# V scaled when it comes back for the spatial product, in odd tiles; two operands of the output weights kept raw and split in phase two; the slots set anew

## The chip, the cores and the metric

One core of a Trainium2 chip runs one launch of the kernel. The metric is the device time of that launch in microseconds. Three runs of the kernel before gave 757.01, 755.66 and 757.59; the median is 757.01.

## The reference

One decoder layer on x of 2048 tokens by 1024 channels, in float32. Cut to what matters here:

```python
h = rms_norm(x, pre_norm_g)
a_u, a_v, sq, sk, sv, mq, z = split(h @ w_in)          # 512, 512, 256, 128, 128, 256, 1024 columns
# A: spatial gating; per token and group of 128 channels
vg = (gelu(a_v) - mean) * rsqrt(var + EPS) * v_g + v_b
sv = einsum('gts,bnsgc->bntgc', tril(w_s), vg) + b_s    # chunks of 128 tokens, 4 groups
y_a = gelu(a_u) * sv
y_b = sliding_window_attention(sq, sk, sv, sinks, rel_bias)   # 4 heads, window 128
y_c = memory_cross_attention(mq, mem_k, mem_v)                # 4 heads, 256 memory tokens
y = concat(y_a, y_b, y_c) * silu(z)
out = x + rms_norm(y @ w_out, post_norm_g)
```

## The kernel before

Every float32 product is made of three products of rounded parts: an operand `w` is kept as a rounded part (ScalarE's cast) and the rest (VectorE's subtraction), and TensorE adds up rounded times rounded and the two cross terms. The helper `split` (lines 144 to 148) makes the two parts; a half-megabyte block of weights thus becomes a megabyte.

**Phase one** takes the tokens in four tiles of 512 (t = 0 to 3). A tile projects V (four products into four PSUM banks, line 1133), then the values and keys of the window attention, q, the memory q and half of the gates z (`group`, line 443). The weights come through a ring of three buffers, loaded already split from DRAM (`split_d`, line 242) after the first tile. After V, line 1151 applies gelu, `bn_stats` gathers mean and variance of each token and group, `scale_and_shift` (lines 296 to 305) turns them into a scale `rv` and a shift `nb` (with a power on GpSimd, line 302), and 16 ScalarE instructions of 128x128 per tile (line 1158) apply them; the result goes to DRAM as `vhat_d` (line 1160). The copy of the values out of PSUM (line 1181) comes after that.

The odd tiles end with `set_a`: a Strassen scheme over two tiles and two blocks of columns makes u and half of z for both tiles at once (28 products of 12 matmuls, line 878). In between, `ahead` loads V back from DRAM for one tile and group (line 857), and `spatial` multiplies it with the spatial weights (`mix`, line 844).

**The output weights.** In tile 2, `weight_operands` loads the four blocks of the output weights, for each half j, makes the seven operands of a second Strassen scheme (B11, T1, B22, T3, T2, B21, T4), splits each in two 512-column pieces (lines 763 to 764) and stores the 2 MB of each operand (both halves) to `wo_d`. T4 is the difference of block 21 and T2; B21 is block 21 itself.

**Phase two** (from line 1243) multiplies y by these operands, two tiles at a time, seven products in each pass, each of four steps (m) of 12 matmuls (line 1443). `work` holds, by step, what else is to be done: loads of y and of operands (`weights`, line 1356), sums, and the splits of y (`rounded` on ScalarE, line 1295, ahead of the bank's own work; `rest` on VectorE, line 1300, behind it). In the first pass the third product, at steps 8 to 11, uses B21, and the sixth, at steps 20 to 23, uses T4.

**What sets the order.** TensorE's and SyncE's (DMA) queues run in program order. In phase one the other engines' order comes from the scheduler's simulated time line. Phase one is cut into slots of six large matmuls (`slot`, line 1036); slot 0 of a tile comes after V, the values, the keys and the first q, 28 slots into the tile. The tables at the head of the file say at which slot of its tile each job is written into the program: MIX_SLOTS (load and spatial product), A_STARTS, A_TURN, A_END (the three stages of each attention unit), WO_SLOTS and WO_LOADS (output weights), H_SUMS, H_LOADS, H_OPS (operands of the first Strassen scheme), and others. In phase two all queues are in program order.

Of the kernel before, what the change touches and what calls it, by code (L numbers as in the profile page):

```python
# [32 lines left out]
W_OPS = ("B11", "B21", "B22", "T1", "T2", "T3", "T4")  # L33
STORE_AFTER = 5

LATE = ((U_Z + 6, 0), (U_Z + 7, 0), (U_V, 1), (U_V + 1, 1), (U_V + 2, 1))

TURN_SLOT = 21

PRE = 28  # L40
N_SLOTS = (36, 84, 28, 84)
BASE = tuple(sum(N_SLOTS[:t]) + PRE * (t + 1) for t in range(NT))
STATS = ((-10, -4, 3, 2, 5, 5, 8, 10), (18, 24, 28, 30, 31, 38, 39, 41), (-22, -20, -17, -10, -9, -5, -2, 1))
SQUARES = ((2, 2, 6, 10, 9, 14, 14, 15),
           (19, 25, 31, 33, 35, 42, 41, 46),
           (-21, -14, -15, -10, -4, -3, 4, 2))
RSTD = ((15, 22, 23), (50, 55, 55), (6, 10, 12))
# [3 lines left out]
LOADS = ((22, 23, 17, 31, 33), (65, 66, 66, 66, 67), (4, 10, 18, 19, 24, 23, 28, 31))
MAKES = ((29, 30, 30, 32, 31, 31, 44, 36),
         (69, 68, 69, 76, 76, 78, 89, 90),
         (16, 16, 21, 22, 24, 25, 30, 36))
A_STARTS = ((10, 16, 21, 26, 35, 38, 41, 44, 47, 50, 53, 58),
# [3 lines left out]
A_TURN = ((6, 8, 11, 8, 11, 8, 5, 8, 10, 9, 11, 6),  # L59
# [3 lines left out]
A_END = ((13, 13, 14, 13, 17, 10, 11, 11, 8, 11, 9, 11),  # L63
# [3 lines left out]

# [6 lines left out]
SEQ_A = tuple((op, g) for op in FIRST_OPS for g in range(4)) + LAST_SEQ  # L74
MIX_SLOTS = ((51, 58), (49, 61), (59, 63), (62, 68), (62, 70), (67, 73), (68, 74), (73, 80))
W_ORDER = ("B11", "T1", "B22", "T3", "T2", "B21", "T4")
WO_SLOTS = ((4, 13, 13, 15, 18, 21, 29), (34, 41, 46, 51, 58, 63, 68))
WO_LOADS = ((-1, 3, 2, 16), (31, 29, 33, 56))
T_SLOTS = (-24, -13, -9, 4)
T_TILES = (1, 1, 1, 1)  # L80
T_STEPS = ((1, 4, 4, 8, 8), (2, 8, 8, 9, 10), (0, 2, 6, 8, 9), (3, 5, 7, 9, 9))
H_SUMS = (((-15, -14, -13, -15, -9, -7, -13, -7, -7, -6, -5),
# [7 lines left out]
H_SPARE = ((-8, 6), (22, 25))  # L90
H_LOADS = (((28, 30, 32, 37), (43, 47, 47, 48), (44, 47, 49, 53)),
           ((33, 37, 38, 35), (33, 39, 38, 41), (49, 49, 46, 56)))
H_OPS = (((35, 38, 37, 42), (54, 56, 53, 54), (51, 56, 53, 63)),
         ((36, 37, 42, 42), (48, 52, 53, 55), (56, 56, 57, 63)))
H_STORE = (3, 3)
Y_SUMS = ((-18, -11, -10), (-15, -8, -7))
Y_OPS = ((66, 73, 67, 79, 70), (72, 80, 80, 79, 80))
Y_WEIGHTS = (63, 81)
VALUES = (5, -4, 1, 0)
PUT_OFF = (4, 0, 3, 7, 6, 4)  # L100


@with_exitstack
def kernel(
# [33 lines left out]
    def f32(ap):  # L138
        return ap.bitcast(F32)
# [65 lines left out]
    vhat_d = dram.tile([NT, 4, P, TS], F32, name="vhat_d")  # L205
    wo_d = {op: dram.tile([2, P, 2, D], F32, name=f"wo_{op}") for op in W_OPS}
    yd = dram.tile([NT, KC, P, TS], F32, name="yd")
# [29 lines left out]
    def split_unit(i):  # L237
# [57 lines left out]
    def scale_and_shift(st, t):  # L295

        twice, apart, spread, rv = (tiny.tile([P, 16], F32, tag=f"v{n}", name=f"v{n}_{t}", bufs=1) for n in ("sum", "dif", "var", "rstd"))
        nc.vector.tensor_tensor(apart, st[:, :, 1], st[:, :, 4], ALU.subtract)
        nc.vector.scalar_tensor_tensor(spread, st[:, :, 2], P * EPS, st[:, :, 5], ALU.add, ALU.add)
        nc.vector.scalar_tensor_tensor(apart, apart, 0.25, apart, ALU.mult, ALU.mult)  # L300
        nc.vector.scalar_tensor_tensor(spread, spread, 1.0 / P, apart, ALU.mult, ALU.add)
        nc.gpsimd.tensor_tensor(rv, spread, mhalf, ALU.pow)
        nc.vector.tensor_tensor(twice, st[:, :, 1], st[:, :, 4], ALU.add)
        nc.vector.scalar_tensor_tensor(twice, twice, -0.5, rv, ALU.mult, ALU.mult)
        return rv, twice
# [442 lines left out]
    def weight_operands(j):  # L748

        r = {}  # L750
        places = ((lambda: quarter(0, 0), lambda: quarter(0, 1), lambda: quarter(1, 0), lambda: quarter(1, 1),
                   lambda: new_spare(0), lambda: new_spare(1), lambda: spare[0]),
                  (lambda: spare[1], lambda: spare[0]) * 4)[j]

# [4 lines left out]
        def operand(op, raw):  # L759
# [4 lines left out]
            store_later(wo_d[op][j], f32(w), PUT_OFF[0])  # L764

        def difference(new, a, b, at):
            r[new] = r[at]
            for c in (slice(0, 512), slice(512, D)):
                nc.vector.tensor_tensor(r[new][:, c], r[a][:, c], r[b][:, c], ALU.subtract)
# [78 lines left out]
    def set_a(p):  # L848
# [6 lines left out]
        def ahead(t, g):  # L855
            vg[t, g] = sp.tile([P, 4, P], F32, tag="L", name=f"vg_{t}_{g}", bufs=4)
            nc.sync.dma_start(vg[t, g], vhat_d[t, :, :, g * P : (g + 1) * P].rearrange("i p c -> p i c"))

        def spatial(t, g):
            gate[t, g] = sp.tile([P, TS], F32, tag="a", name=f"a_{t}_{g}", bufs=3)  # L860
            mix(t, g, vg.pop((t, g)), gate[t, g])
            if t == t1:
                times(U[g], gate[t, g])

        for n, (load_at, mix_at) in enumerate(MIX_SLOTS):
            t, g = (t1, t0)[n % 2], n // 2
            add_jobs(t1, [(load_at, lambda t=t, g=g: ahead(t, g)), (mix_at, lambda t=t, g=g: spatial(t, g))])

# [219 lines left out]
    for t in range(NT):  # L1088
# [58 lines left out]
        st = tiny.tile([P, 16, 6], F32, tag="st", name=f"st_{t}", bufs=1)  # L1147
        Gs = []
        for i in range(4):
            G = sp.tile([P, TS], F32, tag=("G", "ZB")[i // 2], name=f"G_v{t}_{i}", bufs=2)  # L1150
            gelu(vps[i], f"v{t}_{i}", G, 1.0 if t else late["rstd"][:, i : i + 1])
            for g in range(4):
                nc.vector.bn_stats(st[:, 4 * i + g, :], G[:, g * P : (g + 1) * P])
            Gs.append(G)
        rv, nb = scale_and_shift(st, t)
        for i, G in enumerate(Gs):
            for g in range(4):
                nc.scalar.activation(G[:, g * P : (g + 1) * P], G[:, g * P : (g + 1) * P], AF.Identity,  # L1158
                                     bias=nb[:, 4 * i + g : 4 * i + g + 1], scale=rv[:, 4 * i + g : 4 * i + g + 1])
# [437 lines left out]
```

## Time and profile before

| | |
|---|---|
| median of three runs | 757.01 us |
| the profiled execution | 753.89 us |
| its span, first to last instruction | 752.2 us |
| TensorE busy | 736.2 us (98%) |
| VectorE (DVE) busy | 563.8 us (75%) |
| ScalarE (ACT) busy | 475.0 us (63%) |
| GpSimd (POOL) busy | 82.8 us (11%) |
| moved by DMA | 219.92 MB, 292 GB/s over the span |

Times are microseconds from the span's start. PE is TensorE's matmuls, PEld its weight loads, SPq the DMA issues of SyncE. A row of a timeline gives the start, the duration, engine, line, operation, output and inputs, shapes, how many instructions were merged, and in brackets how long the engine was idle before it and what ended that. A row of a group gives the number of instructions, busy time, the mean duration in ns, and the idle time ahead of them.

### The profile page before, as it was taken

The page shows a single profiled execution, that of the slowest core. Times are in us where ns is not written, and L with a number is a line of the kernel's source. Part 1 is how long each engine was busy: PE and PEld are TensorE (multiplying, and loading weights), DVE is VectorE, ACT ScalarE, POOL GpSimd, SP SyncE. Part 2 cuts the span into 40 slices and gives each one's busy share as a digit, 9 for nine tenths or more (in the row PEclk, how much of TensorE's full clock was granted, in tenths as well). Part 3 has the DMA queues.
Part 4 walks back from the last instruction along what each step waited for, and adds up shares of the span by engine and source line. Part 5 has one row for each costly group of instructions (what it writes and reads, how often), then busy time and mean ns, then how long its engine had stood idle before and what let it go on. Part 6 is the DMA issues. An engine that isn't in the chain of part 4 may idle for free.

```text
span 752.2 us, 10609 instructions
## 1 busy us (share of the span) xinstructions
PE 736.2 (98%) x3612; PEld 617.3 (82%) x3612; DVE 563.8 (75%) x1001; ACT 475.0 (63%) x1044; POOL 82.8 (11%) x106
## 2 busy tenths in 40 slices
PE   8999999989999999999999999999999999999996
PEld 6888888768888888887888888888888888888884
DVE  6656897598987589833798968787689528687587
ACT  7799765885599953327668895678954234444441
POOL 1020031100230000010033010221000000010011
PEclk9999999999999999999999999999999999999999
DMA  8989877799975686899998999956577899546924
GB/s 332 360 305 392 292 308 277 272 390 384 341 271 168 221 250 199 293 373 383 367 383 320 393 306 386 377 178 192 170 254 234 284 386 404 184 174 258 352 86 195
DMA packets 80342, 219.92 MB, mean 292 GB/s; under 512 B 7548, under 2 KB 16289, under 8 KB 71841
## 3 DMA queue, kind: packets, MB, share of 16 engines
q1 hardware_dynamic: 75152, 210.27, 77.0%
q10 hardware_dynamic: 5136, 8.98, 3.2%
q8 instruction: 28, 0.46, 0.3%
q14 instruction: 26, 0.20, 0.1%
HBM read 153.16 MB, written 66.07 MB: 291 GB/s over the span
## 4 chain that ended last, share of the span: by engine, by line
PE 71%; DVE 13%; ACT 7%; DMA 6%; issue 1%; POOL 1%; ACTq 0%; DVEq 0%; SPq 0%; POOLq 0%
PE X L878 12%; PE X L1443 12%; PE g_z L443 8%; PE Y_S L1443 6%; PE v L1133 5%; PE g_mq L443 4%; PE Y L878 3%; PE g_q L443 3%; PE Y L1443 3%; ACT G_v L1158 2%; DMA s4b<-in_wst 2%; PE o_b L664 2%; PE gm L555 2%; PE l_b L632 2%; PE Z L878 1%; DVE hs L146 1%
## 5 line engine op out<-in xcount | busy, mean ns | idle before, releaser
L443 PE MATMUL g_z<-hs,ring 128*128 128x512 f32 x360 | 87.6, 394 | 0.0
L1133 PE MATMUL v<-ring,hs 128*128 128x512 f32 x336 | 81.4, 393 | 0.2 <-ACT hs L399 0.2
L443 PEld LDWEIGHTS g_z<-hs,ring 128*128 128x128 f32 x360 | 66.0, 188 | 12.7
L1133 PEld LDWEIGHTS v<-ring,hs 128*128 128x128 f32 x336 | 61.6, 188 | 13.6 <-ACT ring L145 0.6
L878 PE MATMUL X<-hs,ring 128*128 128x512 f32 x288 | 71.1, 394 | 0.0
L878 PEld LDWEIGHTS X<-hs,ring 128*128 128x128 f32 x288 | 52.6, 188 | 10.0
L443 PE MATMUL g_q<-hs,ring 128*128 128x512 f32 x192 | 46.8, 396 | 0.0
L443 PE MATMUL g_mq<-hs,ring 128*128 128x512 f32 x192 | 45.5, 391 | 0.7 <-DMA ring<-split_d 0.7
L443 PEld LDWEIGHTS g_mq<-hs,ring 128*128 128x128 f32 x192 | 35.5, 188 | 8.1 <-DMA ring<-split_d 1.1
L443 PEld LDWEIGHTS g_q<-hs,ring 128*128 128x128 f32 x192 | 35.8, 190 | 7.1
L146 DVE TENSOR_TENSOR ring<-wraw_a,ring 128x1024 fp32r<-128x1024 f32 x28 | 34.4, 1229 | 8.6 <-ACT ring L145 6.6
L1336 POOL TENSOR_TENSOR r<-a,mhalf 128x1 f32<-128x1 f32 x16 | 12.8, 801 | 221.0 <-DVE a L1334 216.3
L654 POOL TENSOR_SCALAR_AFFINE_SELECT pT_b<-pT_b 128x512 fp32r<-128x512 f32 x30 | 21.9, 730 | 133.3 <-ACT pT_b L145 133.3
L1443 PE MATMUL Y_S<-hs,yop 128*128 128x512 f32 x144 | 33.1, 389 | 0.0
L610 ACT ACTIVATE L_c<-L_c,den_c 128x256 f32<-128x256 f32 x64 | 29.1, 507 | 5.1 <-DVE den_c L608 5.1
L1443 PEld LDWEIGHTS Y_S<-hs,yop 128*128 128x128 f32 x144 | 27.0, 188 | 5.6
L146 DVE TENSOR_TENSOR ring<-wraw,ring 128x1024 fp32r<-128x1024 f32 (+1 forms) x18 | 20.9, 1162 | 13.9 <-ACT ring L145 13.7
L1304 ACT ACTIVATE junk<-oa 128x512 f32<-128x512 f32 x16 | 10.1, 633 | 33.5 <-DVE oa L1490 24.6
L1443 PE MATMUL X<-hs,ring 128*128 128x512 f32 x120 | 30.7, 391 | 0.0
L1443 PE MATMUL X<-hs,yop 128*128 128x512 f32 x120 | 30.5, 390 | 0.0
L1300 DVE TENSOR_TENSOR yop<-y,yop 128x1024 fp32r<-128x1024 f32 x10 | 12.2, 1222 | 24.0 <-ACT yop L1295 24.0
L145 ACT CAST ring<-wraw_a 128x1024 fp32r<-128x1024 f32 x28 | 29.3, 1046 | 0.0
(285 smaller groups left out, 1776.3 us busy)
## 6 DMA issues: line engine op xcount, KB each, us to landing
ring<-split_d SPq DMA_DIRECT2D x38, 1024.0 KB, 8.2
split_d<-ring SPq DMA_DIRECT2D x12, 1024.0 KB, 9.4
wraw<-in_wst SPq DMA_DIRECT2D x21, 512.0 KB, 5.8
hs<-wo_B SPq DMA_DIRECT2D x8, 1024.0 KB, 8.3
y<-yd SPq DMA_DIRECT2D x8, 1024.0 KB, 11.1
xs<-in_x SPq DMA_DIRECT2D x24, 256.0 KB, 6.7
hd_S<-h SPq DMA_DIRECT2D x24, 256.0 KB, 6.6
hrS<-hd_S SPq DMA_DIRECT2D x24, 256.0 KB, 4.6
```

The lines of the kernel that those rows point to most:

```text
L145: a = nc.scalar.copy(hi, src)
L146: b = (lo_engine or nc.vector).tensor_tensor(lo, src, f32(hi), ALU.subtract)
L443: nc.tensor.matmul(ps, w[:, wi, k * P : (k + 1) * P], h(t, hi, k), start=(n == 0), stop=(n == 3 * KC - 1))
L555: nc.tensor.matmul(ps, w[:, wi, k * P : (k + 1) * P], late["mT"](hi, k), start=(n == 0), stop=(n == 3 * KC - 1))
L610: last = nc.scalar.mul(p[:, e, :], p[:, e, :], den[:, e : e + 1])
L632: nc.tensor.matmul(lg[:, e, :], S[kv][:, e, c * P : (c + 1) * P], keys[t][:, kv, s, c * P : c * P + 256], start=(s == 0), stop=(s == 1))
L654: nc.gpsimd.affine_select(prev[:, s], f32(own[:, s]), [[0, 4], [-1, P]], ALU.is_gt, 0.0, base=0, channel_multiplier=1)
L664: nc.tensor.matmul(o[:, kv, :], SV[:, c + w, kv].rearrange("p a b -> p (a b)"), pT, start=(n == 0), stop=(n == len(terms) - 1))
L878: nc.tensor.matmul(banks[g], w[:, wi, k * P : k * P + P], at_slot(places[op], hi, k), start=first and i == 0, stop=i == 11, skip_group_che ...
L1133: nc.tensor.matmul(vps[i], h(t, hi, 2 * j + kk)[:, i * P : (i + 1) * P], w[:, wi, kk * 512 : (kk + 1) * 512], start=(j == 0 and (hi, wi, k ...
L1158: nc.scalar.activation(G[:, g * P : (g + 1) * P], G[:, g * P : (g + 1) * P], AF.Identity, bias=nb[:, 4 * i + g : 4 * i + g + 1], scale=rv[ ...
L1443: nc.tensor.matmul(banks[m], a(s, k)[:, m * P : (m + 1) * P], w(v, k), start=first and n == 0, stop=n == 11, skip_group_check=not first)
```

## The change

*V.* After gelu the tile is stored to `vhat_d` as it is. `scale_and_shift` is called after that, and its two results are kept (`moments`, with two buffers). The 16 scalings of line 1158 go from each tile; in the odd tiles a job `centred` between the load and the spatial product makes four of them for each tile and group, on the tile that was loaded back. MIX_SLOTS gets a third slot for it.

*The output weights.* B21 and T4 are no longer split in tile 2. Block 21 is copied inside DRAM at slot 45 of tile 1 (`worw_d["B21"]`, 1 MB), and the difference T4 is stored raw (1 MB). In phase two each of the two is loaded raw into the place of the rest, rounded into its own place by ScalarE, and the rest is made in place by VectorE, in two halves: B21 at steps 3 and 4, T4 at steps 17 and 18.

*Slots.* The tables of slots are set anew, some by one or two, some by more, and a store is issued six slots after it is written instead of five.

```diff
-STORE_AFTER = 5
+STORE_AFTER = 6
...
-A_END = ((13, 13, 14, 13, 17, 10, 11, 11, 8, 11, 9, 11),
-         (16, 15, 14, 16, 8, 11, 9, 11, 12, 9, 10, 11),
-         (14, 14, 13, 14, 14, 11, 9, 11, 11, 10, 10, 14),
-         (13, 13, 15, 16, 19, 14, 12, 14, 14, 12, 4, 11))
+A_END = ((14, 14, 15, 14, 18, 10, 18, 14, 10, 13, 9, 12),
+         (16, 15, 14, 16, 8, 11, 12, 12, 12, 10, 10, 11),
+         (16, 14, 13, 14, 18, 11, 9, 11, 11, 11, 10, 14),
+         (13, 13, 15, 16, 20, 13, 12, 15, 18, 12, 7, 11))
...
-MIX_SLOTS = ((51, 58), (49, 61), (59, 63), (62, 68), (62, 70), (67, 73), (68, 74), (73, 80))
-W_ORDER = ("B11", "T1", "B22", "T3", "T2", "B21", "T4")
-WO_SLOTS = ((4, 13, 13, 15, 18, 21, 29), (34, 41, 46, 51, 58, 63, 68))
-WO_LOADS = ((-1, 3, 2, 16), (31, 29, 33, 56))
+MIX_SLOTS = ((53, 56, 58),
+             (49, 59, 61),
+             (58, 61, 62),
+             (62, 63, 67),
+             (62, 68, 70),
+             (67, 67, 73),
+             (68, 72, 75),
+             (73, 77, 79))
+W_ORDER = ("B11", "T1", "B22", "T3", "T2")
+LATE_OPS = ("B21", "T4")
+COPY_SLOT = 45
+WO_SLOTS = ((4, 13, 13, 15, 17, 21), (35, 41, 49, 51, 58, 57))
+WO_LOADS = ((-1, 3, 2, 17), (31, 29, 33, 55))
...
-H_LOADS = (((28, 30, 32, 37), (43, 47, 47, 48), (44, 47, 49, 53)),
+H_LOADS = (((28, 26, 35, 39), (40, 43, 47, 42), (47, 48, 47, 54)),
...
-    wo_d = {op: dram.tile([2, P, 2, D], F32, name=f"wo_{op}") for op in W_OPS}
+    wo_d = {op: dram.tile([2, P, 2, D], F32, name=f"wo_{op}") for op in W_ORDER}
+    worw_d = {op: dram.tile([2, P, D], F32, name=f"worw_{op}") for op in LATE_OPS}
...
+        def whole(op):
+            store_later(worw_d[op][j], r[op], PUT_OFF[0])
...
-                [lambda: operand("B21", "21"), lambda: difference("T4", "21", "T2", "21")],
-                [lambda: operand("T4", "T4")]]
+                [lambda: difference("T4", "21", "T2", "21"), lambda: whole("T4")]]
...
+        def centred(t, g):
+            rv, nb = moments[t]
+            for i in range(4):
+                c = slice(4 * i + g, 4 * i + g + 1)
+                nc.scalar.activation(vg[t, g][:, i, :], vg[t, g][:, i, :], AF.Identity, bias=nb[:, c], scale=rv[:, c])
...
-            add_jobs(t1, [(load_at, lambda t=t, g=g: ahead(t, g)), (mix_at, lambda t=t, g=g: spatial(t, g))])
+            add_jobs(t1, [(load_at, lambda t=t, g=g: ahead(t, g)), (scale_at, lambda t=t, g=g: centred(t, g)),
+                          (mix_at, lambda t=t, g=g: spatial(t, g))])
...
+            add_jobs(t, [(COPY_SLOT, lambda: nc.sync.dma_start(worw_d["B21"], wst[U_O + 2 : U_O + 4]))])
...
-            Gs.append(G)
-        rv, nb = scale_and_shift(st, t)
-        for i, G in enumerate(Gs):
-            for g in range(4):
-                nc.scalar.activation(G[:, g * P : (g + 1) * P], G[:, g * P : (g + 1) * P], AF.Identity,
-                                     bias=nb[:, 4 * i + g : 4 * i + g + 1], scale=rv[:, 4 * i + g : 4 * i + g + 1])
             nc.scalar.dma_start(vhat_d[t, i], G)
+        moments[t] = scale_and_shift(st, t)
...
+    def place_half(i, s, j):
+        return spare[j][:, s] if i == SPARE else quarter(i, j)[:, s]
+
     def weights(op, i):
-        load_operand(op, i)
         B[op] = slot_rows(i)
+        if op not in LATE_OPS:
+            load_operand(op, i)
+            return
+        for j in range(2):
+            nc.sync.dma_start(f32(place_half(i, 1, j)), worw_d[op][j])
+
+    def weights_rounded(i, j):
+        nc.scalar.copy(place_half(i, 0, j), f32(place_half(i, 1, j)))
+
+    def weights_rest(i, j):
+        lower = place_half(i, 1, j)
+        nc.vector.tensor_tensor(lower, f32(lower), f32(place_half(i, 0, j)), ALU.subtract)
+
+    def late_weights(op, i, s, *steps):
+        at(s, weights, op, i)
+        for j, step in enumerate(steps):
+            at(step, weights_rounded, i, j)
+            at(step, weights_rest, i, j)
...
-    at(0, weights, "B21", SPARE)
+    late_weights("B21", SPARE, 0, 3, 4)
...
-    at(8, weights, "T4", 2)
+    late_weights("T4", 2, 8, 17, 18)
...
-            if (f is rounded) == now:
+            if (f in (rounded, weights_rounded)) == now:
```

More of the change, by code (lines that the diff above doesn't have):

```diff
@@ L33 @@
 W_OPS = ("B11", "B21", "B22", "T1", "T2", "T3", "T4")
-STORE_AFTER = 5
+STORE_AFTER = 6
 LATE = ((U_Z + 6, 0), (U_Z + 7, 0), (U_V, 1), (U_V + 1, 1), (U_V + 2, 1))
-TURN_SLOT = 21
+TURN_SLOT = 26
 PRE = 28
@@ L42 @@
 BASE = tuple(sum(N_SLOTS[:t]) + PRE * (t + 1) for t in range(NT))
[L43 to L47, printed above, removed]
+STATS = ((-6, 0, 6, 6, 8, 9, 10, 14), (18, 24, 27, 27, 33, 38, 39, 41), (-20, -16, -15, -10, -7, -3, 2, -1))
+SQUARES = ((2, 0, 8, 10, 8, 14, 12, 15), (22, 24, 30, 33, 35, 42, 41, 46), (-17, -14, -15, -10, -3, 0, 2, 0))
+RSTD = ((17, 24, 22), (50, 53, 54), (4, 11, 16))
 LOAD_HOMES = ((((0,), "xk"), ((1,), "xk"), ((2, 3, 4, 5), "s4b"), ((6,), "e"), ((7,), "e")),
@@ L50 @@
               tuple(((k,), "xk") for k in range(8)))
[L51 to L55, printed above, removed]
[3 rows of a table removed]
-A_TURN = ((6, 8, 11, 8, 11, 8, 5, 8, 10, 9, 11, 6),
[3 rows of a table removed]
-A_END = ((13, 13, 14, 13, 17, 10, 11, 11, 8, 11, 9, 11),
[3 rows of a table removed]
+LOADS = ((18, 25, 15, 29, 31), (66, 67, 66, 64, 68), (8, 10, 18, 19, 24, 23, 28, 31))
+MAKES = ((29, 30, 30, 32, 33, 29, 42, 36),
+         (70, 66, 67, 73, 76, 76, 90, 88),
+         (16, 16, 21, 22, 24, 25, 34, 33))
+A_STARTS = ((10, 16, 18, 26, 35, 38, 41, 41, 47, 50, 56, 58),
[3 rows of a table added]
+A_TURN = ((7, 10, 11, 8, 11, 8, 5, 8, 10, 9, 11, 9),
[3 rows of a table added]
+A_END = ((14, 14, 15, 14, 18, 10, 18, 14, 10, 13, 9, 12),
[3 rows of a table added]
 H_AT = ((0, 1), (2, 3), (2, 3), (0, 1))
@@ L74 @@
 SEQ_A = tuple((op, g) for op in FIRST_OPS for g in range(4)) + LAST_SEQ
-MIX_SLOTS = ((51, 58), (49, 61), (59, 63), (62, 68), (62, 70), (67, 73), (68, 74), (73, 80))
-W_ORDER = ("B11", "T1", "B22", "T3", "T2", "B21", "T4")
-WO_SLOTS = ((4, 13, 13, 15, 18, 21, 29), (34, 41, 46, 51, 58, 63, 68))
-WO_LOADS = ((-1, 3, 2, 16), (31, 29, 33, 56))
-T_SLOTS = (-24, -13, -9, 4)
-T_TILES = (1, 1, 1, 1)
-T_STEPS = ((1, 4, 4, 8, 8), (2, 8, 8, 9, 10), (0, 2, 6, 8, 9), (3, 5, 7, 9, 9))
-H_SUMS = (((-15, -14, -13, -15, -9, -7, -13, -7, -7, -6, -5),
[7 rows of a table removed]
-H_SPARE = ((-8, 6), (22, 25))
-H_LOADS = (((28, 30, 32, 37), (43, 47, 47, 48), (44, 47, 49, 53)),
[L92 to L97, printed above, removed]
+MIX_SLOTS = ((53, 56, 58),
[11 more added lines that the diff above has]
+WO_LOADS = ((-1, 3, 2, 17), (31, 29, 33, 55))
+T_SLOTS = (-24, -12, -9, 4)
+T_TILES = (1, 1, 1, 1)
+T_STEPS = ((0, 3, 6, 6, 7), (3, 10, 10, 12, 12), (3, 5, 9, 11, 12), (2, 4, 7, 9, 9))
+H_SUMS = (((-18, -14, -13, -15, -9, -7, -13, -7, -7, -6, -4),
[7 rows of a table added]
+H_SPARE = ((-7, 7), (20, 21))
+H_LOADS = (((28, 26, 35, 39), (40, 43, 47, 42), (47, 48, 47, 54)),
+           ((31, 35, 36, 32), (31, 40, 38, 41), (50, 51, 43, 57)))
+H_OPS = (((35, 38, 36, 42), (52, 54, 54, 53), (49, 54, 50, 61)),
+         ((37, 40, 42, 42), (50, 48, 53, 55), (52, 52, 56, 59)))
+H_STORE = (3, 1)
+Y_SUMS = ((-17, -11, -7), (-7, -2, -1))
+Y_OPS = ((64, 71, 65, 77, 71), (71, 82, 83, 82, 82))
 Y_WEIGHTS = (63, 81)
-VALUES = (5, -4, 1, 0)
-PUT_OFF = (4, 0, 3, 7, 6, 4)
+VALUES = (9, -2, 6, 6)
+PUT_OFF = (5, 0, 0, 8, 6, 4)
 @with_exitstack
@@ L257, in split_unit @@
             stores.append((i, u, w))
+    moments = {}
     raws, loaded, halved, pending = {}, [0], [0], set()
@@ L295, in scale_and_shift @@
     def scale_and_shift(st, t):
-        twice, apart, spread, rv = (tiny.tile([P, 16], F32, tag=f"v{n}", name=f"v{n}_{t}", bufs=1) for n in ("sum", "dif", "var", "rstd"))
+        twice, apart, spread, rv = (tiny.tile([P, 16], F32, tag=f"v{n}", name=f"v{n}_{t}", bufs=2) for n in ("sum", "dif", "var", "rstd"))
         nc.vector.tensor_tensor(apart, st[:, :, 1], st[:, :, 4], ALU.subtract)
@@ L751, in weight_operands @@
         places = ((lambda: quarter(0, 0), lambda: quarter(0, 1), lambda: quarter(1, 0), lambda: quarter(1, 1),
-                   lambda: new_spare(0), lambda: new_spare(1), lambda: spare[0]),
-                  (lambda: spare[1], lambda: spare[0]) * 4)[j]
+                   lambda: new_spare(0)),
+                  (lambda: new_spare(1), lambda: spare[0], lambda: spare[1], lambda: spare[0], lambda: spare[1]))[j]
         def load(block):
@@ L863, in spatial @@
                 times(U[g], gate[t, g])
-        for n, (load_at, mix_at) in enumerate(MIX_SLOTS):
+        for n, (load_at, scale_at, mix_at) in enumerate(MIX_SLOTS):
             t, g = (t1, t0)[n % 2], n // 2
-            add_jobs(t1, [(load_at, lambda t=t, g=g: ahead(t, g)), (mix_at, lambda t=t, g=g: spatial(t, g))])
+            add_jobs(t1, [(load_at, lambda t=t, g=g: ahead(t, g)), (scale_at, lambda t=t, g=g: centred(t, g)),
+                          (mix_at, lambda t=t, g=g: spatial(t, g))])
         def product(n, banks, first, then):
@@ L1147 @@
         st = tiny.tile([P, 16, 6], F32, tag="st", name=f"st_{t}", bufs=1)
-        Gs = []
         for i in range(4):
```

24 rows, old and new, of tables (A_STARTS, A_TURN, H_SUMS) are left out of this document.

## The prediction

> **What bounds the kernel now.** I read the page first, then the waits of TensorE alone, then the timeline around the long ones, then windows by stage for the room on the other engines.
>
> ```profile
> PE 736.2 (98%) x3612; PEld 617.3 (82%) x3612; DVE 563.8 (75%) x1001; ACT 475.0 (63%) x1044; POOL 82.8 (11%) x106
> ```
>
> TensorE is busy for 736.2 of a span of 752.2 us, and the change neither adds nor removes a matmul. So nothing is won by a shorter ACT or DVE sum as such; what can be won is the time in which PE stood still, and what can be lost is new standing. The waits of PE (engine, line, what it waited for: us in total, times, longest) say how much there is:
>
> ```profile
> PE l_c L682 <- ACT svs L1181: 3.3, 1, 3.3
> ...
> PE o_b L664 <- POOL pT_b L656: 1.3, 2, 0.7
> PE g_mq L443 <- DMA ring<-split_d: 0.7, 1, 0.7
> PE l_b L632 <- DVE S_q L597: 0.4, 1, 0.4
> PE tp_b L647 <- DVE OB L669: 0.4, 1, 0.4
> PE g_k L443 <- ACT L_c L692: 0.3, 1, 0.3
> PE o_c L710 <- DVE pT_c L146: 0.2, 1, 0.2
> PE o_b L664 <- POOL pT_b L654: 0.2, 1, 0.2
> ```
>
> Beside the start and the tail, which the change leaves alone, these are 6.8 us (3.3 + 1.3 + 0.7 + 0.4 + 0.4 + 0.3 + 0.2 + 0.2). The long one has a price behind it. Windows give busy time per engine in a stretch; the number after POOL is the granted clock, then DMA share and GB/s:
>
> ```profile
> 155.60:159.10 3.50, 3.50 (x12) 2.83 (x11) 3.44 (x6) 1.76 (x4) 0.00 (x0) 0.51 1.05 414
> ```
>
> Right after the 3.3 us wait TensorE ran 3.5 us at half clock (0.51), which costs another 1.7 us (3.5 x 0.49). So 8.5 us in all can be had, and no more.
>
> Who makes PE wait? First the timeline at 147 us, tile 1:
>
> ```profile
> 147.20 2.42 ACT L1158 ACTIVATE G_v<-G_v,vsum,vrstd 128x128 f32<-128x128 f32 x6 [0.20 <-DVE vsum L304]
> ...
> 154.18 0.56 ACT L1181 COPY svs<-g_sv 128x512 f32<-128x512 f32 x1
> ...
> 154.79 0.74 PE L682 MATMUL l_c<-MK,S_mq 128*128 128x256 f32 x4 [3.33 <-ACT svs L1181]
> ```
>
> From 147.2 on ACT works off the sixteen V scalings of the tile (L1158); the copy that frees a PSUM bank (L1181) is behind them and starts at 154.18, and PE stands until it is done. The same block stands behind two of the smaller waits. In tile 2 its last piece starts at 344.58:
>
> ```profile
> 344.58 1.25 ACT L1158 ACTIVATE G_v<-G_v,vsum,vrstd 128x128 f32<-128x128 f32 x3
> ...
> 346.20 0.63 ACT L361 ACTIVATE xs<-xs 128x512 f32<-128x512 f32 x1
> ...
> 346.94 0.33 SPq L356 DMA_DIRECT2D xs<-in_x  x1
> ...
> 347.38 0.38 SPq L242 DMA_DIRECT2D ring<-split_d  x1
> ```
>
> A square (L361) waits its turn behind the block, the load into that square's buffer (L356) heads SP's queue, and the weight load (L242) goes out only at 347.4; it is the one for which PE waits 0.7 us. In tile 3:
>
> ```profile
> 449.99 1.25 ACT L1158 ACTIVATE G_v<-G_v,vsum,vrstd 128x128 f32<-128x128 f32 x3
> ...
> 458.22 1.29 DVE L146 TENSOR_TENSOR s4a<-wo,s4a 128x512 fp32r<-128x512 f32 x2
> ...
> 460.90 0.51 PE L632 MATMUL l_b<-KK,S_q 128*128 128x256 f32 x2 [0.38 <-DVE S_q L597]
> ```
>
> The heads of q come late on ACT behind the block and then on DVE behind a split of an output-weight block; it is B21, which is no longer split there.
>
> **The change part by part.** *The V block.* What goes, and its price:
>
> ```profile
> L1158 ACT ACTIVATE G_v<-G_v,vsum,vrstd 128x128 f32<-128x128 f32 x64 | 25.1, 481 | 1.9 <-DVE vsum L304 1.9
> ```
>
> 25.1 us for 64, so 6.3 us per tile leave the stretch behind V, with the wait for POOL's power ahead of them. The three waits above go: 3.3 + 1.7 + 0.7 + 0.4 = **6.1 us**. What is late next in tile 1 is that copy itself: with 6.3 us less ahead of it, it starts near 147.9 and is done by 148.5, ahead of the 151.5 (154.79 - 3.33) at which PE came to need it.
>
> *The same 64 instructions come back* in the odd tiles, 32 in each (12.6 us of ACT), four ahead of each spatial product. That is a new wait: `sg` on PE now needs ACT, and PE is in order, so all its later products are behind it; on ACT, whatever follows waits while V is still landing. The room:
>
> ```profile
> 220.00:259.00 39.00, 39.00 (x204) 33.10 (x203) 25.32 (x45) 36.10 (x89) 3.50 (x5) 1.00 0.62 206
> 259.00:306.00 47.00, 47.00 (x245) 40.07 (x243) 41.19 (x65) 23.54 (x38) 0.00 (x0) 1.00 0.70 227
> 500.00:541.00 41.00, 41.00 (x217) 34.74 (x216) 29.14 (x50) 34.58 (x79) 2.79 (x4) 1.00 0.58 188
> 541.00:588.00 47.00, 47.00 (x243) 40.06 (x242) 40.90 (x61) 25.27 (x41) 0.00 (x0) 1.00 0.71 242
> ```
>
> The new slots 53 to 79 lie at about 259 to 304 and 541 to 586 (six large matmuls to a slot, counted along PE's instructions). There ACT is busy 23.54 and 25.27 of 47 us, so 12.6 more fit. Only the first product of each odd tile sits at the edge of a stretch that is 93% and 84% full. Loading V back takes
>
> ```profile
> DMA to landing us min/median/max: 2.9/4.7/9.0
> ```
>
> (the view of tile `vg`), and the slots leave two to ten slots of 1.4 us or more between load and product. Bounds for one product: nothing, or its whole four scalings, 1.6 us (4 x 0.39). I take half of that for the first of each odd tile and nothing for the other fourteen: **+1.6 us**.
>
> *Two operands stay raw.* Tile 2 loses B21 and T4, for both halves, so eight of each of these:
>
> ```profile
> L145 ACT CAST s4b<-wo 128x512 fp32r<-128x512 f32 x10 | 5.7, 616 | 0.0
> ...
> L146 DVE TENSOR_TENSOR s4b<-wo,s4b 128x512 fp32r<-128x512 f32 x10 | 6.5, 686 | 0.4 <-ACT s4b L145 0.3
> ```
>
> 4.9 us of ACT and 5.5 us of DVE, and 3 MB of stores (4 MB become 1). One of the DVE splits is straight ahead of another wait of PE:
>
> ```profile
> 385.35 1.29 DVE L146 TENSOR_TENSOR s4b<-wo,s4b 128x512 fp32r<-128x512 f32 x2 [0.33 <-ACT s4b L145]
> ...
> 388.56 0.63 PE L647 MATMUL tp_b<-ident,Lc_b 128*128 128x128 f32 x4 [0.36 <-DVE OB L669]
> ```
>
> Of the remaining 2.4 us of waits (8.5 - 6.1) some fall to this and to attention ends put a slot later, some may not, and moved slots can make new ones. Bounds: all 2.4 won, or as much lost again. I take half won: **-1.2 us**.
>
> *Phase two gets the splits.* Four casts and four subtractions of 128x1024; the first pair of operands is the urgent one, because the product with B21 starts at 613.85:
>
> ```profile
> 609.09 1.05 ACT L1295 CAST yop<-y 128x1024 fp32r<-128x1024 f32 x1
> ...
> 612.89 1.23 DVE L1300 TENSOR_TENSOR yop<-y,yop 128x1024 fp32r<-128x1024 f32 x1 [1.49 <-ACT yop L1295]
> ...
> 613.85 1.52 PE L1443 MATMUL Y<-s4a,yop 128*128 128x512 f32 x6
> ...
> 615.21 1.52 PE L1443 MATMUL Y<-s4b,yop 128*128 128x512 f32 x6
> ```
>
> ```profile
> 592.00:614.00 22.00, 22.00 (x99) 18.23 (x98) 5.01 (x6) 6.44 (x10) 0.00 (x0) 1.00 0.88 332
> ```
>
> DVE has 17 us free there and ACT 15. The raw load is half as large as the two old ones (0.5 MB each), and loads of that size took
>
> ```profile
> wraw<-in_wst SPq DMA_DIRECT2D x21, 512.0 KB, 5.8
> ```
>
> so about 607 for an issue near 601, and both casts (2 x 1.05) fit ahead of the cast that ran at 609.1 or push it by under 1 us; the second half of y was ready at 614.1 and used at 615.2, so 1.1 us is spare. The second pair (T4) has the time of two whole steps. Cost: **nothing**; without that cover, one cast and one subtraction, 2.3 us.
>
> *Transfers.* If tile 1 runs 5.0 us ahead (3.3 + 1.7), its loads must come sooner, in a stretch where the DMA engines are full:
>
> ```profile
> 160.00:180.00 20.00, 20.00 (x99) 16.68 (x98) 17.07 (x32) 11.27 (x21) 0.90 (x1) 1.00 1.01 390
> 180.00:200.00 20.00, 20.00 (x100) 16.85 (x99) 19.25 (x36) 11.67 (x36) 2.82 (x4) 1.00 0.98 376
> ```
>
> These 40 us moved 15.3 MB. At the 414 GB/s of the quoted half-clock stretch they would take 37.0 us, so up to 3.0 of the 5.0 us are there; stores and loads for the next tile can slip as well. Bounds: nothing, or all 5.0 given back. I take one late weight load like the 0.7 above: **+0.7 us**. Tiles 2 and 3 lose 3 MB, which helps. The copy of B21 inside DRAM (1 MB) falls at slot 45, near 245 us, where the share is 0.62; over all 16 engines at 390 GB/s it is 2.7 us of their idle time: nothing.
>
> **Sum:** -6.1 - 1.2 + 1.6 + 0.7 = -5.0 us. Against the profiled execution (753.9 us, 1.7 of it around the span) that is 748.9. The median of the runs is 757.0, 3.1 above the profiled one, a difference that I carry over: **752.0 us**.
>
> **The rivals.** (1) *Every wait goes and nothing comes back*: 757.0 - 8.5 = 748.5. For it: each wait has a cause that the change touches or moves. Against it: the two full stretches above.
>
> (2) *The DMA engines set the pace of tile 1*: 3.5 us come back there and 2 us at the spatial products, so with 7.3 won (6.1 + 1.2) it is -7.3 + 5.5 = -1.8, 755.2 us, no change. For it: shares of 1.01 and 0.98 for 40 us. Against it: 414 GB/s seen next to them.
>
> (3) *PE waits for the scaling at the spatial products* (slower): DVE is busy 41.19 of 47 us there, tanh and gelu on ACT wait for its sums, and a scaling queued behind one of those makes PE wait too. It decides from 0.46 us for each of 16 products (7.3 / 16). With half of the four scalings uncovered at all of them, 0.8 us each, it is 12.8 - 7.3 = +5.5: 762.5 us. Against it: ACT has 23 us free.
>
> [...]
>
> **How the numbers follow.** Forecast 0.52, (1) 0.16, (2) 0.13, (4) 0.05, (3) and other new waits by moved slots 0.14. A measurement tells about 0.3% (2.3 us) from no change: faster (under 754.7) 0.68, same 0.18, slower (over 759.3) 0.14. The forecast's own range is 749 to 754.5. The range for 8 in 10 goes down to 747.5, one us below (1), and up past (2) to (4), 758.6; it leaves out (3).
>
> **What would show it.** In the changed kernel's waits of PE, the row of `l_c` behind L1181 and the half clock near 155 us are gone, as are the ring load near 354 and `l_b` near 461; new rows, if any, name `sg` behind ACT, with under 2 us in total. Windows in 259 to 306 show ACT near 36 us of 47. In phase two PE has no wait at the product with B21. It is wrong if PE's waits and half clock sum to more than 6 us: then the rows name which rival.

## The result, and the profile after

The changed kernel takes 749.95 us (median of 7 runs, 747.47 to 751.68); the kernel before, on the same chip, 755.54 (7 runs, 752.61 to 757.59). The ratio is 0.9931, with a 95% interval of 0.9905 to 0.9956: 5.6 us faster. A second series, told below, gave 749.37 and a ratio of 0.9928 (0.9908 to 0.9949).

Two executions of the changed kernel were profiled: 751.22 us (span 749.5) and 748.13 us (span 746.4). First the busy time per engine of the first, from its page:

```profile
PE 733.6 (98%) x3612; PEld 615.7 (82%) x3612; DVE 560.2 (75%) x997; ACT 477.9 (64%) x1042; POOL 83.6 (11%) x106
```

ACT's sum rose by 3, DVE's fell by 4: as forecast, no gain lies there. Then the waits of PE (what PE ran next, what it waited for, us in total, times, longest), in the first execution:

```profile
PE g_z L452 <- DMA ring<-split_d: 1.8, 1, 1.8
...
PE tp_c L708 <- DVE pT_c L153: 1.7, 1, 1.7
PE v L1152 <- DMA ring<-split_d: 1.5, 2, 1.3
PE g_mq L452 <- DMA ring<-split_d: 1.3, 1, 1.3
PE o_b L673 <- POOL pT_b L665: 0.5, 1, 0.5
```

and in the second:

```profile
PE tp_c L708 <- DVE pT_c L153: 1.7, 1, 1.7
PE g_mq L452 <- DMA ring<-split_d: 0.9, 1, 0.9
PE l_c L691 <- DVE OC L724: 0.5, 1, 0.5
PE v L1152 <- DMA ring<-split_d: 0.5, 1, 0.5
```

The 3.3 us behind the copy out of PSUM are gone, and so is the half clock behind it. The copy now starts at 145.22, nine microseconds sooner, and the window that stood at 0.51 of the clock stands at 1.00 (a row of windows gives length, busy time of PE, PEld, DVE, ACT and POOL, then the clock, DMA share and GB/s):

```profile
145.22 0.58 ACT L1194 COPY svs<-g_sv 128x512 f32<-128x512 f32 x1
```

```profile
155.60:159.10 3.50, 3.50 (x19) 2.88 (x19) 3.47 (x7) 3.44 (x7) 0.00 (x0) 1.00 1.02 330
...
259.00:306.00 47.00, 47.00 (x244) 40.01 (x243) 41.98 (x68) 33.14 (x63) 0.00 (x0) 1.00 0.67 226
541.00:588.00 47.00, 47.00 (x244) 40.03 (x243) 40.78 (x62) 33.91 (x66) 0.00 (x0) 1.00 0.73 248
```

In the stretches of the spatial products ACT is now busy 33 to 34 of 47 us, and PE still all 47. But new waits stand in the two lists: 1.7 us at the transposes `tp_c` in both, and weight loads that come late, 4.6 us in the first execution and 1.4 in the second. Waits and half clock together were 8.5 us before; they are 6.8 and 3.6 now. The two executions differ by 3.1 us, and the weight loads by 3.2; that is nearly all of it.

### The profile page after: what moved, and what is told of

Its sections match the earlier page's. It is cut to its first block, busy times and chain, and to the rows that moved or that the text cites. A ratio compares the mean times of both kernels' runs of the same rounds, so it can differ in the third digit from the quotient of the medians.

```text
span 749.5 us, 10602 instructions
## 1 busy us (share of the span) xinstructions
PE 733.6 (98%) x3612; PEld 615.7 (82%) x3612; DVE 560.2 (75%) x997; ACT 477.9 (64%) x1042; POOL 83.6 (11%) x106
## 4 chain that ended last, share of the span: by engine, by line
PE 61%; DMA 15%; DVE 9%; ACT 4%; issue 3%; POOL 1%; SPq 0%; DVEq 0%; ACTq 0%; POOLq 0%
PE X L896 12%; PE X L1476 12%; PE Y L896 6%; PE Y_S L1476 6%; PE v L1152 4%; PE g_z L452 3%; PE Z L896 3%; PE Y L1476 3%; DMA ring<-split_d 3%; DMA xs<-in_x 2%; PE sg L855 2%; DMA wraw<-in_wst 2%; PE o_c L719 1%; PE g_mq L452 1%; PE g_q L452 1%
## 5 line engine op out<-in xcount | busy, mean ns | idle before, releaser
L619 ACT ACTIVATE L_c<-L_c,den_c 128x256 f32<-128x256 f32 x64 | 28.9, 507 | 3.3 <-DVE den_c L617 3.3
L650 ACT ACTIVATE Lc_b<-Lc_b,nm_b 128x129 f32<-128x129 f32 x64 | 25.0, 394 | 7.7 <-DVE nm_b L648 7.6
```

Of the source, the lines that this page charges most:

```text
L619: last = nc.scalar.mul(p[:, e, :], p[:, e, :], den[:, e : e + 1])
L650: nc.scalar.activation(Lc[:, h, : P + 1], Lc[:, h, : P + 1], AF.Exp, bias=nm[:, h : h + 1], accum_out=den[:, h : h + 1])
```

## The experiments

The prediction's theory was that the scalings behind the projection are the gain, the weights a microsecond, the slots about nothing. The rival: the slots are the gain. Three parts can be taken alone. "V" is the scaling moved, with the new MIX_SLOTS; "weights" is B21 and T4 kept raw; "slots" is all the tables, the load and product slots of MIX_SLOTS among them. So these slots are in two of the parts. "The old tables" below are all but MIX_SLOTS. All changes below are against the kernel before as it ran on the same chip (its medians were 754.7 to 755.5).

### V alone

```diff
+        moments[t] = scale_and_shift(st, t)          # behind the four stores of V
...
+            add_jobs(t1, [(load_at, ...), (scale_at, lambda t=t, g=g: centred(t, g)), (mix_at, ...)])
 STORE_AFTER = 5                                      # this and all tables but MIX_SLOTS as before
```

> Theory (the leaving of the V block from behind the projection is the gain): this part alone, with the new MIX_SLOTS and every other table of before, gains 3.5 to 6 us (6.1 won less up to 1.6 at the spatial products, and up to 1 for late loads); the waits of PE lose the row of l_c behind L1181, and the clock near 155 us stays at 1.0. Rival (the slots set anew are the gain, and V only moves work): within 2 us of before, and as many us of other waits of PE appear as the row of l_c takes away.

769.43 us against 754.9: **14.5 us slower**, ratio 1.0205 (1.0178 to 1.0232). Neither theory had that. Its waits of PE, the four longest that aren't the start:

```profile
PE o_c L718 <- ACT pT_c L152: 5.9, 3, 4.0
PE g_q L451 <- DMA ring<-split_d: 3.3, 2, 2.6
PE tp_b L655 <- ACT Lc_b L618: 2.0, 1, 2.0
...
PE X L1452 <- DVE ring L1309: 1.6, 1, 1.6
```

The wait of `l_c` in tile 1 is gone, as the theory wanted (the 0.9 us left in its row lie in tile 3, at 451), but PE now stands in the same place for something else. ACT's timeline there (start, duration; ACTq is a DMA issue on ACT's own queue):

```profile
139.31 1.09 ACT L728 ACTIVATE G_v<-v 128x512 f32<-128x512 f32 x2
139.94 2.89 ACTq L1168 DMA_DIRECT2D vhat_d<-G_v  x2
142.88 0.60 ACT L728 ACTIVATE G_v<-v 128x512 f32<-128x512 f32 x1 [2.48 <-PE l_c L690]
145.85 0.33 ACTq L1168 DMA_DIRECT2D vhat_d<-G_v  x1
146.21 1.28 ACT L700 ACT_TABLE_LOAD   x1 [2.73 <-DMA tu_d<-s4b]
...
148.60 0.58 ACT L152 CAST pT_c<-tp_c 128x512 fp32r<-128x512 f32 x1
```

```profile
149.23 2.01 PE L718 MATMUL o_c<-pT_c,MV 128*128 128x512 f32 x4 [4.03 <-ACT pT_c L152]
```

A table load waits 2.73 us for the transfer `tu_d`, the store of an unrelated sum. What it truly waits for is the store of V ahead of it. In the traces each transfer of SyncE's and ScalarE's queues raises one of eight semaphores, taken in turn by both queues (in the kernel before 439 issues, 54 or 55 to each); 393 of these issues first wait on that same semaphore, all sixteen stores of V among them. Such an issue waits until the transfer that used the semaphore last has landed; for thirteen of those sixteen stores it is the eighth before. With V alone:

```
store of V   issued    same semaphore used by    landed
second       139.94    ring<-split_d             139.79
third        142.50    split_d<-ring             142.43
fourth       145.85    tu_d<-s4b                 145.77
```

Of 269 issues of this profile whose predecessor's landing is fully recorded, none left earlier than that landing, and 26 left within 0.15 us of it (17 in the kernel before). In the changed kernel the fourth store of the same tile left at 140.81, 0.07 us behind the landing of `tu_d` (140.74) on its semaphore. SyncE has only issues to make, so such a stop on its queue held back transfers alone. On ScalarE's queue it stopped ScalarE: the last gelu above stood 2.48 us and the table load 2.73, with the casts behind them. With the time of the gelu itself taken off, the sixteen stores of V stopped ScalarE for 11.9 us in this kernel, 5.9 of them at 347 us; in the kernel before, where they were issued some 10 us later behind the scalings, for next to nothing; in the changed kernel for 0.3, with 1.6 us more in two issues of its first tile that took 1.0 and 1.2 us themselves, where most take 0.33.

### Weights alone, slots alone, and both parts without the slots

> The two operands kept raw, alone, with the other tables of before. Theory: between 0 and 1.5 us faster, not to be told from no change; the row of l_c behind L1181 (3.3 us) and the half clock stay; PE has no wait at the third product of phase two (B21), and the copy inside DRAM lands within 10 us. Rival (the copy or the late splits cost): 1.5 us or more slower than before, with a wait of PE on B21's rest, or on transposes near 263 us.

759.68, **4.8 us slower**, ratio 1.0062 (1.0041 to 1.0083). The wait and the half clock stay, as expected. The time is on the rival's side, but neither of the rival's waits is there (on B21's rest, at the transposes near 263). What came is in tile 3 and in the clock: two waits of `l_b` behind the heads of q make 2.7 us (0.4 before), with splits of output weights ahead of those heads on DVE, and the half clock behind `l_c` lasts 6.8 us and not 3.4, which costs another 1.7. Why it lasted twice as long isn't shown.

> All tables of after, but V scaled behind the projection and all seven operands split in tile 2, as before. Theory: within 2.5 us of before, because the 3.3 us behind L1181 and the half clock are caused by the sixteen scalings, which stay in their place. Rival (the slots are the gain): 3 to 6 us faster than before.

764.55, **9.6 us slower**, ratio 1.0130 (1.0112 to 1.0148). In these slots the sixteen scalings of tile 1 do their harm at another victim: they stand ahead of the cast and the activation (`L_c`) that the transposes' chain needs.

```profile
150.64 3.95 ACT L1157 ACTIVATE G_v<-G_v,vsum,vrstd 128x128 f32<-128x128 f32 x10
154.62 0.59 ACT L143 CAST pT_c<-tp_c 128x512 fp32r<-128x512 f32 x1
```

```profile
PE tp_c L698 <- ACT L_c L691: 4.1, 1, 4.1
PE l_b L631 <- DVE S_q L596: 3.7, 2, 3.2
PE g_mq L442 <- DMA ring<-split_d: 3.0, 1, 3.0
```

That wait of 4.1 us with its half clock takes the place of the 3.3 with its own, and so adds only 0.8. The loss lies elsewhere: `l_b` in tile 3, for which the heads of q come late on DVE, and a weight load in tile 2, each with a half clock behind it that the kernel before didn't have. Together these two add some 9 us.

> Both parts, with the tables of before apart from MIX_SLOTS and the entry that T4 loses in WO_SLOTS. Theory: 4 to 7 us faster than before, as fast as after within 2 us. Rival (the slots are the gain): at least 3 us slower than after. If the parts are independent, its gain is the sum of the two alone.

768.28, **13.4 us slower**, ratio 1.0176 (1.0156 to 1.0196). The stores of V stop ScalarE for 11.6 us here too. So the same work costs 768.3 us with the old tables and 750 with the new ones, while the new tables with the old work cost 764.6. Neither theory holds in its simple form: the gain belongs to no part alone, the three together are 5.6 us faster where their single effects sum to 28.9 us slower.

### Each part put back

Against the changed kernel:

```diff
-        moments[t] = scale_and_shift(st, t)
+        rv, nb = scale_and_shift(st, t)              # and the sixteen scalings ahead of the stores
```

> The kernel after, with V scaled behind the projection again, as before; weights and all slots as after. Theory of the prediction (the V block is the gain): 4 to 8 us slower than after, with a wait of over 2 us behind the sixteen scalings near 150 us. Rival (slots and work belong together, and any part put back costs by what it collides with): over 8 us slower than after. Rival (the V part is worth nothing): within 2 us of after.

758.44 us, ratio to before 1.0047 (1.0023 to 1.0070): some 9 us slower than the changed kernel. By the time this is about 1 us on the first rival's side; the wait that the theory named is there as well. The old block makes 5.7 of it, a wait of 4.0 now at the transposes, as with the slots alone, and its half clock; weight loads, one of them with a half clock of its own, make most of the rest:

```profile
PE tp_c L701 <- ACT L_c L694: 4.0, 1, 4.0
PE g_mq L445 <- DMA ring<-split_d: 2.9, 1, 2.9
PE v L1138 <- DMA ring<-split_d: 2.1, 1, 2.1
```

```diff
-W_ORDER = ("B11", "T1", "B22", "T3", "T2")
+W_ORDER = ("B11", "T1", "B22", "T3", "T2", "B21", "T4")   # split in tile 2, no copy of block 21
```

> The kernel after, with B21 and T4 split in tile 2 again and loaded as two parts, as before; V and all slots as after. Theory of the prediction (this part is worth about 1 us at most): 0 to 2 us slower than after. Rival (slots and work belong together): 3 us or more slower than after, with new waits of PE in tile 2 or 3.

754.46 us, ratio to before 0.9999 (0.9980 to 1.0019): some 5 us slower than the changed kernel, on the rival's side. But 3 us of them (a wait of 1.3 and a half clock of 1.7) don't lie in tile 2 or 3. They lie in tile 1, ahead of any work that was put back:

```profile
251.14 1.65 ACT L869 ACTIVATE vg<-vg,vsum,vrstd 128x128 f32<-128x128 f32 x4 [2.90 <-DMA vg<-vhat_d]
252.70 0.56 ACT L150 CAST pT_c<-tp_c 128x512 fp32r<-128x512 f32 x1
```

In the changed kernel this cast runs at 249.27, and the scalings come behind it and other work, at 254.34. Here the scalings are first, ACT stands 2.9 us until V has landed, and all that follows is 3.4 us late, the cast of the next unit too, for which PE stands at 257.41. The written slots of this tile are the same in both kernels. The order on ACT in phase one comes from the simulated time line; the one thing that this edit takes away ahead of that place is the copy inside DRAM (slot 45 of that tile). That it turned the order is argued, not shown.

### The stores of V on another queue

```diff
-            nc.scalar.dma_start(vhat_d[t, i], G)
+            nc.gpsimd.dma_start(vhat_d[t, i], G)
```

> The V part alone as in v_only, but its sixteen stores of V are issued on GpSimd's queue and not on ScalarE's. New theory (queue): V alone lost 14.5 us because these stores, now written right behind each gelu, stop ScalarE until the transfer eight issues earlier has landed (15 us of such stops in the trace of v_only, the longest 6.5 us). Then ScalarE's stops go and at least 6 of the 14.5 us come back (763 us or less); the wait of o_c near 149 us (4.0 us) and that of tp_b near 399 us go. Rival (slots: the spatial products, the attention stages and the loads of before don't suit the moved work): it stays within 4 us of v_only, 765 to 773 us.

761.44 us, ratio 1.0096 (1.0070 to 1.0122): 8.0 of the 14.5 us came back. (The 15 us in the expectation still held the gelu's own time; 11.9 is the figure, and 5.9 the longest.) Both waits named are gone, PE enters `o_c` at 145.36 without standing; the `o_c` row that is left lies at 259 and 274:

```profile
PE g_q L451 <- DMA ring<-split_d: 6.5, 3, 2.7
...
PE o_c L718 <- ACT pT_c L152: 1.7, 2, 1.2
```

What is left is mostly weight loads that come late, which this edit didn't touch. The edit also takes the issuing itself, 0.33 us a store, off ScalarE and sixteen transfers off the two queues that share the eight semaphores; what each of these is worth wasn't separated from the stops. The same edit in the changed kernel:

> The kernel after, with the stores of V issued on GpSimd's queue. [...] Rival (GpSimd's own work, the power and the copies of keys and values, comes late behind the stores): 1 us or more slower than after, with waits of PE behind GpSimd or behind the moments.

747.48 us, ratio 0.9908 (0.9889 to 0.9928). It is clearly faster than the kernel before (7.6 us), but its interval overlaps that of the changed kernel, 0.9905 to 0.9956: a gain over it can't be told. (The stops at semaphores that this edit takes away are 0.3 us in the changed kernel.) What it does show is what the 1.7 us at `tp_c` hang on. On DVE, in the changed kernel:

```profile
147.62 0.17 DVE L313 SCALAR_TENSOR_TENSOR vsum<-vsum,vrstd 128x16 f32<-128x16 f32 x1 [1.58 <-POOL vrstd L311]
...
151.68 0.68 DVE L153 TENSOR_TENSOR pT_c<-tp_c,pT_c 128x512 fp32r<-128x512 f32 x1
```

and with the stores on GpSimd's queue:

```profile
146.56 0.18 DVE L313 SCALAR_TENSOR_TENSOR vsum<-vsum,vrstd 128x16 f32<-128x16 f32 x1 [1.60 <-POOL vrstd L311]
...
150.57 0.69 DVE L153 TENSOR_TENSOR pT_c<-tp_c,pT_c 128x512 fp32r<-128x512 f32 x1
```

```profile
PE tp_c L708 <- DVE pT_c L153: 0.6, 1, 0.6
```

The moments of V, now wanted only 100 us later, still stop DVE 1.6 us for GpSimd's power; behind them DVE has no pause up to the subtraction that the transposes' next user needs. Here the whole row comes 1.1 us sooner, and PE's wait falls by 1.1 us. That the stop of 1.6 us is the cause of the wait is argued from these rows; moving the moments themselves was not tried.

### Twice the work ahead of the spatial products

```diff
                 nc.scalar.activation(vg[t, g][:, i, :], vg[t, g][:, i, :], AF.Identity, bias=nb[:, c], scale=rv[:, c])
+                nc.scalar.copy(vg[t, g][:, i, :], vg[t, g][:, i, :])
```

> The kernel after, in which each of the four scalings ahead of a spatial product is followed by a copy of the same 128x128 in place on ScalarE, so that 3.2 us and not 1.6 lie between V's landing and the product, and 25 us more of ScalarE's work in the odd tiles. Theory of the prediction (that work lies in free time): within 2 us of after, with at most two waits of sg behind ScalarE. Rival 3 of the prediction (PE waits for the scalings at the products): 0.8 us or more at each of 16 products, so 10 us or more slower than after.

761.97 us, ratio to before 1.0105 (1.0088 to 1.0123), 12 to 13 us slower than the changed kernel. The time is that of rival 3, and so is the mechanism, but not at all products: there are four waits, two at the first product of each odd tile, with one half clock behind each pair.

```profile
PE sg L855 <- ACT vg L875: 6.4, 4, 2.2
PE g_mq L452 <- ACT S_q L605: 2.0, 1, 2.0
```

```profile
266.57 0.49 PE L855 MATMUL sg<-wsp,vg 128*128 128x128 f32 x2 [2.04 <-ACT vg L875]
268.68 1.65 PE L855 MATMUL sg<-wsp,vg 128*128 128x128 f32 x6 [1.63 <-ACT vg L875]
```

```profile
260.43 0.51 ACT L875 COPY vg<-vg 128x128 f32<-128x128 f32 x2
265.41 0.30 ACT L875 COPY vg<-vg 128x128 f32<-128x128 f32 x1
266.22 0.29 ACT L875 COPY vg<-vg 128x128 f32<-128x128 f32 x1
268.31 0.91 ACT L875 COPY vg<-vg 128x128 f32<-128x128 f32 x4
```

Four copies need 1.2 us; the first four took 6.1 us, because other work of ACT came between them. So rival 3 was right that PE waits where the work ahead of a product is queued behind something. Its price and places were not: some 3 us at two products, not 0.8 at sixteen. In the changed kernel no product waits: its list has no `sg`. Waits and half clock at `sg` make 9.8 us. The `g_mq` row, 2.0 us, lies at 358 in tile 2, where nothing was added; what made it isn't shown. How much more work the place would bear, this run doesn't measure.

### Two attempts to gain more

```diff
-Y_SUMS = ((-17, -11, -7), (-7, -2, -1))
+Y_SUMS = ((-18, -11, -10), (-15, -8, -7))            # and V's stores on GpSimd's queue
```

> V's stores on GpSimd's queue as in after_pool, and the slots of the y sums (loads of 1.5 MB of the first gates) set as before, ((-18, -11, -10), (-15, -8, -7)). Theory (the second of these loads, moved from slot -15 to -7 by the change, is ahead of the ring load for which PE waits near 351 us): that wait of g_mq (3.0 us in after_pool, 1.3 in after) and the half clock behind it go, 2 to 5 us faster than after_pool. Rival (the DMA engines are full there in any order): the same sum of waits behind ring loads, within 1.5 us of after_pool.

751.34 us, ratio 0.9959 (0.9942 to 0.9976): slower than with the stores alone, not faster. The wait of `g_mq` did go, and another of the same length came at the weight load before it, with its half clock:

```profile
PE g_q L452 <- DMA ring<-split_d: 3.4, 1, 3.4
```

The rival's mechanism holds: waits behind ring loads sum to 5.1 us, against 3.0 with the stores alone. Its bound of 1.5 us does not, the run is 3.9 us slower than that one. Around 340 us the DMA engines are full, in the second profile of the changed kernel too:

```profile
326.00:360.00 34.00, 33.07 (x152) 27.21 (x151) 18.19 (x45) 16.31 (x32) 3.51 (x2) 1.00 1.03 402
```

That the order of the loads then chooses which weight load is late fits these rows; no other order was tried.

```diff
-            nc.sync.dma_start(s[1], s[2])
+            nc.gpsimd.dma_start(s[1], s[2])              # all deferred stores of phase one, beside the edit above
```

> As pool_y, and all deferred stores of phase one (gates, operands, sums) are issued on GpSimd's queue instead of SyncE's. Theory (queue): SyncE's loads no longer have to wait until stores issued up to eight transfers earlier have landed, so the ring loads go out sooner; faster than pool_y by 0 to 3 us. Rival (GpSimd's own work, the masks of the window attention, is on PE's path and comes late behind stores that wait for their data): slower than pool_y by 2 us or more, with waits of PE at o_b behind GpSimd.

771.6 us, ratio 1.0230 (1.0201 to 1.0259): 20 us slower than the one before it. GpSimd's sum rose from 90.4 to 135.0 us, and PE waited for its masks:

```profile
PE g_q L452 <- DMA ring<-split_d: 4.9, 1, 4.9
...
PE o_b L673 <- POOL pT_b L665: 2.2, 3, 1.6
```

The rival named these waits, but they are the smaller part: 3.0 of 17.1 us of PE's waits are for GpSimd's masks (in the run before this one all waits are 5.7). What made the others longer isn't shown.

### The changed kernel once more

> The kernel after once more, for a second profile and more timings. If the waits behind ring loads (4.6 us in four places in the first profile) belong to the program, the same places (187.8, 351.5 and 402.1 us, within 2 us) wait again with 3 to 6 us in total; if they are chance of one execution, other places wait or the total is under 2 us. Time against before: 4 to 7 us faster; after_pool (7.6 us faster) stays within 3 us of it, so that the two can't be told apart.

749.37 us (748.13 to 750.62). Of the three places where weights came late, 187.8 was gone; near 350 and at the start of tile 3 (391 in place of 402) PE waited 0.9 and 0.5. By the bound of the expectation (1.4 us, under 2) this is chance of one execution. The other runs say more: the wait near 188 is there again with the copies added (1.85 at 188.1) and with the weights put back (1.34 at 188.2), and between 340 and 358 PE waits for a weight load in every run of the new tables but the one with the copies. So the places recur, and their size changes from run to run; one profile can't tell what a place costs.

## Why the prediction was right, and where it was not

Forecast -5.0 us, measured -5.6 and -6.0. The forecast time of 752.0 was 2 us high, 1.5 of it because it started from the first three runs of the kernel before, whose median was 757.0; with four further runs it is 755.5. The sum, term by term, in the two profiles:

```
term of the sum                            forecast   first   second
V block: l_c behind the copy, half clock     -5.0      -5.0    -5.0
  weight load of tile 2 (g_mq)               -0.7      +0.6    +0.2
  l_b behind the heads of q                  -0.4      -0.4    -0.4
the remaining 2.4 us                         -1.2      -1.9    -2.4
late weight loads elsewhere                  +0.7      +3.3    +0.5
scalings at the spatial products             +1.6       0       0
tp_c, l_c behind DVE in tile 1                0        +1.7    +2.2
sum                                          -5.0      -1.7    -4.9
```

The profiled executions are 2.7 and 5.8 us below that of before, each 0.9 to 1.0 more than its waits explain. (The profiled execution of before was 1.7 us under its median, the first of the changed kernel 1.3 over its own.) That the total agrees so well is in part luck: the +1.6 for the scalings came out at nothing, and a wait that no term had, 1.7 to 2.2 us, took its place.

*Right:* the block behind the projection and its half clock; the scalings hidden between load and product; phase two. B21 lands in time, its casts start at 603.93, and PE runs into its product without a wait:

```profile
603.93 1.05 ACT L1381 CAST s4a<-s4a 128x1024 fp32r<-128x1024 f32 x1 [2.63 <-DMA s4a<-worw_B]
```

No run shows the term (4), 758.6 us, to which the range goes up. What the trace shows of the copy inside DRAM: it was issued at 239.92 and ran as sixteen packets of 65,536 bytes, 2.42 to 2.67 us long, between 243.7 and 247.2, all sixteen under way at once at 244.7.

*Wrong in the sum:* "What is late next in tile 1 is that copy itself". Late next was a subtraction on DVE: 1.7 us in both profiles. It runs behind the moments of V, which the change left where they were. The prediction had "the wait for POOL's power" leave with the scalings; it left ScalarE, but on DVE it stayed, 1.29 us before and 1.58 after. And "the three waits above go" failed for the weight load of tile 2: the load is issued at 339.31 and no longer at 347.38, but into full DMA engines (busy share 1.03 from 326 to 360), where it took 12.0 us, and PE waits for it 0.9 to 1.3 us where it waited 0.7. One reading was off without harm: between load and product the new table has 4 to 12 slots, not two to ten.

*Wrong by a step left out:* "The V block. What goes" counted the sixteen scalings and not the sixteen stores behind them, which move to the gelus on ScalarE's own queue. Nothing was priced for them and no rival named them. In the changed kernel they stop ScalarE for 0.3 us; with the old tables for 11.9 us, and 8 us of time came back when they left its queue.

*Mis-sized most:* "moved slots can make new ones. Bounds: all 2.4 won, or as much lost again". The tables are worth 18 us to this work (768.3 to 750). The forecast came out near the result because it assumed that the new order would neither stop ScalarE nor starve PE, and no number of it showed that; the runs did.

The prediction called itself wrong if PE's waits and half clock passed 6 us. One of two profiles passes (6.8, with 4.6 of weight loads, rival (2) in small), the other doesn't (3.6).

## What to carry to other kernels

When work leaves an engine's queue, list every instruction that moves up with it, DMA issues above all: here an issue stood up to 5.9 us for a transfer that has nothing to do with it, and on ScalarE's queue the work behind it stood too. In a kernel whose order is set by tables, a part tried alone with the old tables says little about the part: here each of three was slower alone and all three together were faster. Read waits from two profiles before a wait of a microsecond is given a cause.

## What the runs showed of the hardware and of the program

*Eight semaphores for two queues.* The issues on SyncE's and ScalarE's queues share eight semaphores (439 issues in the kernel before, 438 in the changed one), and issues stood for an unrelated transfer alone (5.9 us at 347 with V alone). This is in the program's own waits, and so a property of how it is put together rather than of the chip.

*A half clock behind a wait of 1.34 us, none behind one of 1.83.* In the kernel before, the granted clock is 0.50 from 155.66 for 3.413 us, behind the wait of 3.33 us. In the changed kernel the longest wait between the start and the tail, 1.83 us up to 187.84, has no half clock behind it: the clock stands at 1.00 from 5.3 to 746.0. But with the weights put back a wait of 1.34 us was followed by one: the eleven matmuls of the last row took 4.27 us, and eleven of the usual distances of 0.227 us make 2.5:

```profile
257.41 0.73 PE L716 MATMUL o_c<-pT_c,MV 128*128 128x512 f32 x2 [1.34 <-ACT pT_c L150]
258.32 0.73 PE L716 MATMUL o_c<-pT_c,MV 128*128 128x512 f32 x2 [0.18 <-DVE pT_c L151]
258.89 4.27 PE L891 MATMUL X<-hs,ring 128*128 128x512 f32 x11
```

Count as standing the time by which a matmul starts later than the usual distance behind the one before it (0.227 us for 512 columns, 0.120 for 256, 0.109 for 128), where that is over 0.1 us. In the profile of before the four changes of the clock lie 44, 1 and 173 times 3.413 us apart, and the two in the first of the changed kernel 217 times, each to 0.1 us. With these two profiles cut into stretches of 3.413 us at those places, PE stood for 2.65 us of the one ahead of the half clock; in the others, the start and the tail apart, for at most 1.36 us before and 1.72 after. What length of standing brings a half clock isn't shown. What ends one stays open too: that of the weights alone lasted 6.8 us.
